# Twelve products instead of six to each addition in a squared-ReLU MLP

## The chip, the cores and the metric

The kernel runs on one core of a Trainium2 chip. Its time is the device time of one execution in microseconds (us); the figure of a kernel is the median of several executions. One execution is also taken by the hardware profiler, and its trace is what the views below are read from. The engines are PE (TensorE: matmuls; PEld is its loading of stationary operands), DVE (VectorE), ACT (ScalarE), POOL (GpSimd) and SP (SyncE, whose queue issues all DMAs here).

## The reference

One layer of a streaming encoder for 2048 prompt tokens and 32 sample tokens, model width 1024:

```python
def ffn_ple(h, p, g_mlp, w_up, w_down, w_ple_gate, w_ple_proj):
    c = rmsnorm(h, g_mlp)
    h = h + jnp.square(jax.nn.relu(c @ w_up)) @ w_down
    return h + jax.nn.sigmoid(h @ w_ple_gate) * (p @ w_ple_proj)
```

Ahead of it stand an RMSNorm, one input projection, two groups of attention heads (group A: differential attention over chunk-causal keys, group B: a band of nine chunks) and the output projection with its residual. After it comes a final RMSNorm. Everything is float32. `w_up` is 1024 x 4096 and `w_down` 4096 x 1024, so d_ff is 32 tiles of 128 and the width is 8 tiles of 128.

## The kernel before, in words

**Precision.** Each float32 operand is split into a high part (rounded to fp32r, by ACT: `wh`, `uh`, `cH`) and a low part (the difference, by POOL or DVE: `wl`, `ul`, `cL`). A product takes three matmuls: high by high, high by low, low by high (`mm3`, lines 256 to 262). These three lines, 260 to 262, stand for nearly all matmuls in the profile; the tiles tell them apart: `ups` for up products, `dps` for down products, `ops` for the output projection.

**Blocks.** The tokens are four blocks: 512, 544 (512 and the 32 sample tokens), 512 and 512. Block 1 is worked as two halves of 272 columns, the others as one of 512 (`SUBS`). Blocks 0 and 1 go through the MLP described here; blocks 2 and 3 go through another form of it later (`uphase`, `dphase`), which the change leaves alone.

**The MLP of a block** (`mlp`, `mlp_up`, `mlp_down`, lines 950 to 1015). d_ff is walked in 16 chunks of two tiles. A chunk's up part takes two weight units of 1024 rows by 128 columns: 24 matmuls for each token half into one PSUM bank, then ReLU and square on ACT (lines 972, 973) into a tile `tmp`, and the split into the two tiles `uh` and `ul`. Its down part takes two weight units of 256 rows by 512 columns. For each of the eight tiles of the width and each token half, six matmuls (two d_ff tiles, three each) go into one PSUM bank, and DVE adds the bank to the residual `h` (line 1001). The down part of a chunk follows the up part of the next one. Ups and downs of the output projection and the norm's sums share one ring of two PSUM banks, `mm`; from chunk 9 of block 1 on, the downs alternate between it and attention's banks.

**Order.** The program is written as generators that are woven together by hand; `mlp` yields after parts of a chunk, and other work (loading and normalizing the next block, the output projections of blocks 2 and 3, and so on) takes a step at each yield. When the kernel is built, a scheduler then lays down a fixed order for each engine from its own estimate of times; so the MLP of blocks 0 and 1, which stands behind attention in the program, fills PE beside the end of attention. On the chip each engine takes its instructions in that fixed order, SP its DMA issues too.

**Rings in SBUF that matter here.** `uq`, eight tiles for `uh` and `ul` (line 1597); `wh` and `wl`, three each, with three raw weight tiles; `tmp` in the pool `wk`, four tiles (`self.nt`, line 201), used for the residual's tiles in the output projection (`hd`, line 870), loads for the norms (`raw_o`, `cload`) and the ReLU's result; `r`, two tiles for the norms' factors (lines 851, 932); a separate `tmp` of seven tiles (`ox`, line 1601) for the work that is woven into block 1, `xnorm2` and `xnorm3` among it (their tiles are called `xe`). A tile of a ring can be taken again when all that read it are done.

Of the kernel before, what the change touches and what calls it, by code (L numbers as in the profile page):

```python
# [12 lines left out]
F32 = mybir.dt.float32  # L13
F32R = mybir.dt.float32r
AF = mybir.ActivationFunctionType
ALU = mybir.AluOpType
# [3 lines left out]
P = 128  # L20
# [69 lines left out]
def packed(w, rows, cols):  # L90
    k = rows // P
    n, m = w.shape[0] // rows, w.shape[1] // cols
    w = w.reshape(n, k, P, m, cols).transpose(0, 3, 2, 1, 4)
    return np.ascontiguousarray(w).reshape(n, m, P, k * cols)


def packed_weights(w):
    v = [w["w_in"][0, :, 1536 * g + 1024 : 1536 * g + 1536] for g in range(2)]
    qk = [w["w_in"][0, :, 1536 * g : 1536 * g + 1024] for g in range(2)]
    return {  # L100
        "w_v": np.stack([packed(x, 512, 256) for x in v]),
        "w_qk": np.stack([packed(x, 1024, P)[0] for x in qk]),
        "w_out": packed(w["w_out"][0], 1024, P)[0],
        "w_up": packed(w["w_up"][0], 1024, P)[0],
        "w_down": packed(w["w_down"][0], 256, 512),
        "w_ple_gate": packed(w["w_ple_gate"][0], 1024, P)[0],
        "w_ple_proj": packed(w["w_ple_proj"][0], 256, 512)[0],
    }
# [17 lines left out]
def drain(gen):  # L126
    for _ in gen:
        pass
# [67 lines left out]
class Kern:  # L196
    def __init__(self, tc, a):
        self.tc = tc
        self.nc = tc.nc
        self.a = a  # L200
        self.nt = 4
        self.nraw = 2
        self.pre = []

# [631 lines left out]
    def oload(self, b, wk, up, out):  # L836
        nc = self.nc
        n, t0 = BN[b], T0[b]
        if up.whole:
            oact = [up.tile([P, 8, up.aw], F32R, tag="act", name="oact") for _ in range(2)]  # L840
            oact = [[t[:, k, :n] for k in range(8)] for t in oact]
        else:
            oact = [[up.tile([P, up.aw], F32R, tag="u", name="ou")[:, :n] for k in range(8)] for _ in range(2)]
        out[b] = oact
        ahead = 1 if type(wk) is Mix else 0
        raws = []
        for k in range(8):
            while len(raws) <= min(k + ahead, 7):
                raws.append(self.raw_o(wk, len(raws), t0, n))
            if k == 4:  # L850
                r = wk.tile([P, BLK], F32, tag="r", bufs=2, name="rb")[:, :n]
                self.dma(r, self.rB[:, t0 : t0 + n])
            raw = raws[k]
            if k >= 4:
                nc.vector.scalar_tensor_tensor(
                    raw, raw, self.g_b[:, k - 4 : k - 3], r, op0=ALU.mult, op1=ALU.mult
                )
            self.split(oact[0][k], oact[1][k], raw, "act", "dve")
            yield
# [65 lines left out]
    def colnorm2(self, sq, b, scale, wk, tp, tag, dst, out):  # L925
        nc = self.nc
        n, t0, subs = BN[b], T0[b], SUBS[b]
        sh = wk.tile([P, BLK], F32R, tag="sh", bufs=1, name="sh")[:, :n]
        sl = wk.tile([P, BLK], F32R, tag="sl", bufs=1, name="sl")[:, :n]
        self.split(sh, sl, sq, "act", "dve")  # L930
        yield
        r = wk.tile([P, BLK], F32, tag="r", bufs=2, name="r")[:, :n]
        for s0, sn in subs:
            ss = tp.tile([P, 512], F32, tag=tag, name="css")[:, :sn]
            nc.tensor.matmul(ss, self.ones, sh[:, s0 : s0 + sn], start=True, stop=False)
            nc.tensor.matmul(ss, self.ones, sl[:, s0 : s0 + sn], start=False, stop=True)
            v = sq[:, s0 : s0 + sn]
            y = r[:, s0 : s0 + sn]
            nc.scalar.activation(v, ss, AF.Copy, scale=scale, bias=EPS)
            nc.scalar.activation(y, v, AF.Ln)  # L940
            nc.scalar.activation(y, y, AF.Exp, scale=-0.5)
            nc.vector.tensor_tensor(v, v, y, op=ALU.mult)
            nc.vector.tensor_tensor(v, v, y, op=ALU.mult)
            nc.vector.tensor_scalar(v, v, -0.5, 1.5, op0=ALU.mult, op1=ALU.add)
            nc.vector.tensor_tensor(y, y, v, op=ALU.mult)
        if dst is not None:
            self.dma(dst[:, t0 : t0 + n], r)
        out.append(r)

    def mlp_up(self, ch, nf, blocks, st, wk, up, mm, lo):  # L950
        nc = self.nc
        us, w = {}, {}
        order = [(f, b) for f in range(nf) for b in blocks]
        if ch == 0:
            order = [(f, b) for b in blocks for f in range(nf)]
        for f, b in order:
            ft = nf * ch + f
            if f not in w:
                w[f] = self.wunit(self.a["w_up"][ft], [8, P], "act", lo)
            wh, wl = w[f]  # L960
            h, cH, cL = st[b]
            uh = up.tile([P, up.aw], F32R, tag="u", name="uh")
            ul = up.tile([P, up.aw], F32R, tag="u", name="ul")
            us[f, b] = (uh, ul)
            for s0, sn in SUBS[b]:
                ps = mm.tile([P, 512], F32, tag="mm", name="ups")[:, :sn]
                self.mm3(
                    ps,
                    [(wh[:, k], wl[:, k], cH[:, k, s0 : s0 + sn], cL[:, k, s0 : s0 + sn]) for k in range(8)],
                )  # L970
                r = wk.tile([P, BLK], F32, tag="tmp", bufs=self.nt, name="relu")[:, :sn]
                nc.scalar.activation(r, ps, AF.Relu)
                nc.scalar.activation(r, r, AF.Square)
                self.split(uh[:, s0 : s0 + sn], ul[:, s0 : s0 + sn], r, "act", lo)
        return us

    def mlp_down(self, ch, nf, blocks, us, st, wk, mm, lo):
        nc = self.nc
        nd = 8 // nf
        for dh in range(nf):  # L980
            wh, wl = self.wunit(self.a["w_down"][ch, dh], [nf, P * nd], "act", lo)
            for d in range(nd):
                dd = nd * dh + d
                for b in blocks:
                    h = st[b][0]
                    for s0, sn in SUBS[b]:
                        ps = mm.tile([P, 512], F32, tag="mm", name="dps")[:, :sn]
                        self.mm3(
                            ps,
                            [  # L990
                                (
                                    wh[:, f, P * d : P * d + P],
                                    wl[:, f, P * d : P * d + P],
                                    us[f, b][0][:, s0 : s0 + sn],
                                    us[f, b][1][:, s0 : s0 + sn],
                                )
                                for f in range(nf)
                            ],
                        )
                        hv = h[dd][:, s0 : s0 + sn]  # L1000
                        nc.vector.tensor_tensor(hv, hv, ps, op=ALU.add)  # L1001
            yield

    def mlp(self, blocks, st, wk, up, mm, md, turn):
        nf = 2
        prev = None
        for ch in range(DFF // (P * nf)):
            lo = "pool" if ch < turn else "dve"
            us = self.mlp_up(ch, nf, blocks, st, wk, up, mm, lo)
            yield ch, 0  # L1010
            if prev is not None:
                for i, _ in enumerate(self.mlp_down(ch - 1, nf, blocks, prev, st, wk, md, lo)):
                    yield ch, 1 + i
            prev = us
        drain(self.mlp_down(ch, nf, blocks, prev, st, wk, md, lo))

    def tsplit(self, dst, src, lo_eng):
        self.split(dst[:, 0], dst[:, 1], src, "act", lo_eng)
# [458 lines left out]
    def run(self):  # L1477
        tc, nc, a = self.tc, self.nc, self.a
        with ExitStack() as top:
# [100 lines left out]
            with ExitStack() as x:  # L1580
                pool = opened(x, "a1", 1, side="right")
                for js in JA1:
                    self.attn_a(js, pool, ps_s, ps_t, ps_o)
            wk = opened(sq_, "wk", 1)
            acc, cn, st = {}, {}, {}
            def norms(b, act, ps):
# [7 lines left out]
                weave(self.outproj(0, wk, oa[0], mm, acc[0]), self.oload(1, wk, oq, oa), 1, 0, OW)  # L1594
                weave(self.outproj(1, wk, oa[1], mm, acc[1]), norms(0, actq, mm), 1, 1)
            hq = opened(sq_, "hq", 1)
            uq = Sized(opened(sq_, "uq", 8), BLK)
            rxs, oxs = ExitStack(), ExitStack()
            rx = Sized(opened(rxs, "rx", 5, side="right"), 512, True)
            ox = opened(oxs, "ox", 1, side="right")  # L1600
            wx = Mix(wk, tmp=(ox, 7))
            ps2 = Rings((ps_t, "tp"))
            X = {}

# [30 lines left out]
            for b in HALVES[0]:  # L1635
# [2 lines left out]
                h = [hq.tile([P, BLK], F32, tag="h", bufs=8, name="h") for _ in range(8)]  # L1638
                hmove(b, h, True)
                dn = Turn(mm)  # L1640
                m = self.mlp((b,), {b: (h,) + cn[b]}, wk, uq, mm, dn, (16, 11)[b])
                if b == 0:
                    next(m)
                    pre = self.cpre(1, wk, self.colnorm(acc[1][0], 1, 1.0 / D, wk, mm, "mm", None))
# [131 lines left out]
```

## Time and profile before

| | us |
|---|---|
| median of 3 runs | 2969.64 (2968.85 to 2970.52) |
| profiled execution | 2970.7 |
| its span, from first to last instruction | 2968.9 |

The granted TensorE clock was 0.994 of full speed over the span. A group's row in the profile reads: line, engine, operation, output <- inputs, shapes, count, then busy us and mean ns of one instruction, then the engine's idle time before the group's instructions and what ended it. A wait's row reads: who waited, for whom, us in total, times, longest. Ends of matmuls are modelled; their starts are measured.

### The profile page before, as it was taken

How to read it: one execution, taken by the hardware profiler on the slowest of the kernel's cores; microseconds unless marked ns; L12 is line 12 of the kernel's file. 1: busy time of each engine (PE TensorE's matmuls, PEld its weight loads, DVE VectorE, ACT ScalarE, POOL GpSimd, SP SyncE). 2: the span in 40 equal slices, each digit the busy share in tenths (PEclk: the TensorE clock that was granted, in tenths of full speed). 3: DMA queues.
4: the chain of work that ended last, by engine and by line, in shares of the span. 5: the costliest groups of instructions: out<-in, count | busy, mean ns of one | idle time of the engine just before them, and what ended most of it. 6: DMA issues, size and time to landing. Idle time of an engine off the chain costs nothing.

```text
span 2968.9 us, 49388 instructions
## 1 busy us (share of the span) xinstructions
PE 2902.3 (98%) x17027; PEld 2556.1 (86%) x17027; DVE 1847.5 (62%) x4120; ACT 1766.0 (59%) x3743; POOL 1386.8 (47%) x1903
## 2 busy tenths in 40 slices
PE   7899999999999999999999999999999999999998
PEld 6798998998889788888899999889888887888886
DVE  6565855444466554776767664376666666777955
ACT  5566757766567665776677764343444454455554
POOL 4677665533355445665564457620755533143000
PEclk9999999999999999999999999999999999999999
DMA  9877577876677644554654325563444486756711
GB/s 360 293 246 240 191 247 262 256 235 196 220 260 243 214 140 163 160 177 151 202 178 152 114 93 170 179 209 111 165 153 156 147 320 224 261 198 203 264 64 57
DMA packets 301370, 584.58 MB, mean 197 GB/s; under 512 B 34720, under 2 KB 132128, under 8 KB 301120
## 3 DMA queue, kind: packets, MB, share of 16 engines
q1 hardware_dynamic: 301120, 581.43, 58.5%
q8 instruction: 135, 2.21, 0.3%
q14 instruction: 115, 0.94, 0.1%
HBM read 450.10 MB, written 131.22 MB: 196 GB/s over the span
## 4 chain that ended last, share of the span: by engine, by line
PE 89%; DVE 5%; DMA 2%; ACT 2%; issue 1%; POOL 1%; SPq 0%; ACTq 0%; DVEq 0%; POOLq 0%
PE ups L260 4%; PE ups L261 4%; PE ups L262 4%; PE qps L261 4%; PE qps L260 4%; PE s L590 4%; PE qps L262 4%; PE dp L260 4%; PE dp L261 4%; PE dp L262 4%; PE dps L260 4%; PE xps L262 3%; PE xps L261 3%; PE xps L260 3%; PE dps L262 3%; PE dps L261 3%
## 5 line engine op out<-in xcount | busy, mean ns | idle before, releaser
L229 POOL TENSOR_TENSOR wl<-wr,wh 128x256 fp32r<-128x256 f32 x736 | 552.1, 781 | 527.2 <-ACT wh L234 458.9
L234 ACT ACTIVATE wh<-wr 128x1024 fp32r<-128x1024 f32 x270 | 284.9, 1056 | 229.6 <-PE dps L261 52.6
L260 PE MATMUL dps<-uh,wh 128*128 128x272 f32 (+1 forms) x768 | 255.6, 333 | 11.2 <-DVE h L1001 10.2
L260 PE MATMUL ups<-cH,wh 128*128 128x272 f32 (+1 forms) x768 | 249.7, 325 | 0.6 <-DVE h L1001 0.5
L261 PE MATMUL ups<-cL,wh 128*128 128x272 f32 (+1 forms) x768 | 249.1, 324 | 0.0
L262 PE MATMUL ups<-cH,wl 128*128 128x272 f32 (+1 forms) x768 | 249.1, 324 | 0.0
L262 PE MATMUL dps<-uh,wl 128*128 128x272 f32 (+1 forms) x768 | 247.9, 323 | 0.0
L261 PE MATMUL dps<-ul,wh 128*128 128x272 f32 (+1 forms) x768 | 247.5, 322 | 0.0
L1001 DVE TENSOR_TENSOR h<-h,dps 128x272 f32<-128x272 f32 (+1 forms) x384 | 194.9, 516 | 73.8 <-PE dps L262 72.0
L260 PE MATMUL qps<-aH,wh 128*128 128x512 f32 (+3 forms) x640 | 228.8, 358 | 0.0
L261 PE MATMUL qps<-aL,wh 128*128 128x512 f32 (+3 forms) x640 | 227.9, 356 | 0.0
L262 PE MATMUL qps<-aH,wl 128*128 128x512 f32 (+3 forms) x640 | 227.6, 356 | 0.0
L219 POOL TENSOR_TENSOR wl<-wr,wh 128x256 fp32r<-128x256 f32 x208 | 154.2, 773 | 118.5 <-ACT wh L234 115.4
L261 PE MATMUL dp<-dx,dw 128*128 128x512 f32 x448 | 178.1, 397 | 0.0
L590 PE MATMUL s<-ka,q 128*128 128x512 f32 (+3 forms) x640 | 174.5, 367 | 2.1 <-DVE nm L599 0.8
L262 PE MATMUL dp<-dx,dw 128*128 128x512 f32 x448 | 175.2, 397 | 0.0
L260 PE MATMUL dp<-dx,dw 128*128 128x512 f32 x448 | 167.7, 398 | 4.6 <-ACT dx L234 4.6
L260 PEld LDWEIGHTS dps<-uh,wh 128*128 128x128 f32 x768 | 144.3, 188 | 30.2 <-DVE h L1001 19.1
L771 DVE CUSTOM_DVE_ANT_0 eb<-sb,bb 128x320 f32<-128x320 f32 (+2 forms) x232 | 104.3, 479 | 99.0 <-PE tpb L783 97.0
L1114 POOL TENSOR_TENSOR wc<-wq,wc 128x256 fp32r<-128x256 f32 x96 | 91.8, 977 | 157.2 <-ACT wc L1111 157.1
L260 PE MATMUL vps<-wh,aH 128*128 128x256 f32 (+1 forms) x544 | 156.6, 290 | 6.5 <-ACT aH L234 5.1
L673 DVE TENSOR_TENSOR pL<-tpp,pH 128x512 fp32r<-128x512 f32 (+5 forms) x168 | 95.9, 584 | 100.4 <-ACT pH L672 99.4
(269 smaller groups left out, 9222.6 us busy)
## 6 DMA issues: line engine op xcount, KB each, us to landing
wd<-w_down SPq DMA_DIRECT2D x96, 512.0 KB, 5.3
q<-qS SPq DMA_DIRECT2D x128, 256.0 KB, 4.0
v<-vSa SPq DMA_DIRECT2D x64, 512.0 KB, 4.0
wr<-w_up SPq DMA_DIRECT2D x64, 512.0 KB, 3.7
wr<-w_down SPq DMA_DIRECT2D x64, 512.0 KB, 3.7
wr<-w_qk SPq DMA_DIRECT2D x58, 512.0 KB, 4.7
ut<-uS SPq DMA_DIRECT2D x56, 512.0 KB, 4.3
qS<-qk SPq DMA_DIRECT2D x32, 512.0 KB, 3.7
```

Of the source, the lines that this page charges most:

```text
L219: nc.gpsimd.tensor_tensor(out[:, sl], a[:, sl], b[:, sl], op=op)
L229: nc.gpsimd.tensor_tensor(out[:, sl], a[:, sl], b[:, sl], op=op)
L234: nc.scalar.activation(hi, raw, AF.Copy)
L260: nc.tensor.matmul(ps, lh, rh, start=start and i == 0, stop=False)
L261: nc.tensor.matmul(ps, lh, rl, start=False, stop=False)
L262: nc.tensor.matmul(ps, ll, rh, start=False, stop=stop and i == n - 1)
L590: nc.tensor.matmul(s, q[:, m, hl, P * qi : P * qi + nr], kt[:, m, k0 - kb : k0 - kb + n], start=hl == 0, stop=hl == 1)
L673: nc.vector.tensor_tensor(l_, s_, h_.bitcast(F32), op=ALU.subtract)
L771: nc.vector.tensor_tensor_reduce(e[:, w * i : w * i + w], s, bb[:nr, b0 + w * i : b0 + w * i + w], 1.0, -3e38, ALU.add, ALU.max, st[:, 3 + ...
L1001: nc.vector.tensor_tensor(hv, hv, ps, op=ALU.add)
L1114: nc.gpsimd.tensor_tensor(w[:, 1, sl], src[:, sl], w[:, 0, sl].bitcast(F32), op=ALU.subtract)
```

## The change

The MLP of a block is worked by four d_ff tiles at a time. A down group has 12 matmuls (four d_ff tiles, three each) before DVE adds its bank to `h`. The down weights are packed a second time, as units of 512 rows by 256 columns (`w_down4`; `w_down` stays for the later blocks); a unit has 512 KB as before, and a block still takes 32 up and 32 down units. The order is five ups, four downs, then four ups and four downs in turn; at the end three ups and four downs. The yields fall after the same numbers of units as before. The ring of `uh` and `ul` grows from 8 to 10 tiles; in exchange `tmp` shrinks from 4 to 3, `r` from 2 to 1 (both from the output projection of block 0 on) and the separate `tmp` from 7 to 6.

```diff
@@ packed_weights
+        "w_down4": packed(w["w_down"][0], 512, 256),
@@ Kern.__init__
-        self.nt = 4
+        self.nt, self.nr = 4, 2
@@ oload, colnorm2
-                r = wk.tile([P, BLK], F32, tag="r", bufs=2, name="rb")[:, :n]
+                r = wk.tile([P, BLK], F32, tag="r", bufs=self.nr, name="rb")[:, :n]
...
+    def mlp_up(self, f, b, st, wk, up, mm, lo):
+        nc = self.nc
+        wh, wl = self.wunit(self.a["w_up"][f], [8, P], "act", lo)
...
+    def mlp_down(self, c, q, b, us, st, mm, lo):
+        nc = self.nc
+        wh, wl = self.wunit(self.a["w_down4"][c, q], [4, 2 * P], "act", lo)
+        for d in range(2):
+            h = st[0][2 * q + d]
+            sl = slice(P * d, P * d + P)
             for s0, sn in SUBS[b]:
-                ps = mm.tile([P, 512], F32, tag="mm", name="ups")[:, :sn]
+                ps = mm.tile([P, 512], F32, tag="mm", name="dps")[:, :sn]
                 self.mm3(
                     ps,
-                    [(wh[:, k], wl[:, k], cH[:, k, s0 : s0 + sn], cL[:, k, s0 : s0 + sn]) for k in range(8)],
+                    [
+                        (wh[:, f, sl], wl[:, f, sl], us[4 * c + f][0][:, s0 : s0 + sn], us[4 * c + f][1][:, s0 : s0 + sn])
+                        for f in range(4)
+                    ],
                 )
...
+                hv = h[:, s0 : s0 + sn]
+                nc.vector.tensor_tensor(hv, hv, ps, op=ALU.add)
+
+    def mlp(self, b, st, wk, up, mm, md, turn):
+        nf = DFF // P
+        units = [(f, None) for f in range(5)]
+        for c in range(nf // 4):
+            units += [(c, q) for q in range(4)]
+            units += [(f, None) for f in range(4 * c + 5, min(4 * c + 9, nf))]
+        us = {}
+        for i, (x, q) in enumerate(units):
+            ch, part = divmod(i + 2, 4)
             lo = "pool" if ch < turn else "dve"
-            us = self.mlp_up(ch, nf, blocks, st, wk, up, mm, lo)
...
+            if q is None:
+                us[x] = self.mlp_up(x, b, st, wk, up, mm, lo)
+            else:
+                self.mlp_down(x, q, b, us, st, md, lo)
+            if ch < 16 and part and (ch, part) != (0, 2):
+                yield ch, (part - 1) * (ch > 0)
@@ run
+            self.nt, self.nr = 3, 1
             wk = opened(sq_, "wk", 1)
...
-            uq = Sized(opened(sq_, "uq", 8), BLK)
+            uq = Sized(opened(sq_, "uq", 10), BLK)
...
-            wx = Mix(wk, tmp=(ox, 7))
+            wx = Mix(wk, tmp=(ox, 6))
...
-                m = self.mlp((b,), {b: (h,) + cn[b]}, wk, uq, mm, dn, (16, 11)[b])
+                m = self.mlp(b, (h,) + cn[b], wk, uq, mm, dn, (16, 11)[b])
```

More of the change, by code (lines that the diff above doesn't have):

```diff
@@ L931, in colnorm2 @@
         yield
-        r = wk.tile([P, BLK], F32, tag="r", bufs=2, name="r")[:, :n]
+        r = wk.tile([P, BLK], F32, tag="r", bufs=self.nr, name="r")[:, :n]
         for s0, sn in subs:
@@ L948, in colnorm2 @@
         out.append(r)
-    def mlp_up(self, ch, nf, blocks, st, wk, up, mm, lo):
+    def mlp_up(self, f, b, st, wk, up, mm, lo):
         nc = self.nc
[L952 to L964, printed above, removed]
+        wh, wl = self.wunit(self.a["w_up"][f], [8, P], "act", lo)
+        h, cH, cL = st
+        uh = up.tile([P, up.aw], F32R, tag="u", name="uh")
+        ul = up.tile([P, up.aw], F32R, tag="u", name="ul")
+        for s0, sn in SUBS[b]:
+            ps = mm.tile([P, 512], F32, tag="mm", name="ups")[:, :sn]
+            self.mm3(
+                ps,
+                [(wh[:, k], wl[:, k], cH[:, k, s0 : s0 + sn], cL[:, k, s0 : s0 + sn]) for k in range(8)],
+            )
+            r = wk.tile([P, BLK], F32, tag="tmp", bufs=self.nt, name="relu")[:, :sn]
+            nc.scalar.activation(r, ps, AF.Relu)
+            nc.scalar.activation(r, r, AF.Square)
+            self.split(uh[:, s0 : s0 + sn], ul[:, s0 : s0 + sn], r, "act", lo)
+        return uh, ul
@@ L971, in mlp_up @@
[L971 to L1007, printed above, removed]
-            lo = "pool" if ch < turn else "dve"
-            us = self.mlp_up(ch, nf, blocks, st, wk, up, mm, lo)
[L1010 to L1015, printed above, removed]
+                    [
+                        (wh[:, f, sl], wl[:, f, sl], us[4 * c + f][0][:, s0 : s0 + sn], us[4 * c + f][1][:, s0 : s0 + sn])
+                        for f in range(4)
+                    ],
+                )
```

## The prediction

> **What bounds the kernel now.** I read the engine totals first, then the busy time by stretch, then TensorE's waits, then its matmuls by shape.
>
> ```profile
> span 2968.9 us, 49388 instructions
> PE 2902.3 (98%) x17027; PEld 2556.1 (86%) x17027; DVE 1847.5 (62%) x4120; ACT 1766.0 (59%) x3743; POOL 1386.8 (47%) x1903
> ```
>
> PE (TensorE) is busy for 98% of the span, no other engine for more than 62%. An edit that takes work off DVE, ACT or POOL is therefore worth only the PE idle time that this work caused. Columns of the next view: stretch, its length, busy time of PE, PEld, DVE, ACT, POOL, granted clock, DMA share, GB/s.
>
> ```profile
> 815.00:960.00 145.00, 143.02 (x950) 131.76 (x949) 91.38 (x266) 101.84 (x189) 75.76 (x105) 0.99 0.75 249
> 960.00:2090.00 1130.00, 1113.81 (x6945) 1002.57 (x6944) 705.40 (x1530) 695.21 (x1478) 557.88 (x785) 1.00 0.50 162
> 1980.00:2010.00 30.00, 26.46 (x201) 25.15 (x200) 30.00 (x56) 14.65 (x27) 0.00 (x0) 1.00 0.60 195
> ```
>
> The MLP of blocks 0 and 1 runs from 960 to 2090 us, woven with the last of the attention: the program order is one thing, the order laid down at build time fills attention's gaps on PE with MLP matmuls. PE idles 1130 - 1113.8 = 16.2 us there, at a full clock. 3.5 us of it lie in 1980 to 2010, where DVE is busy for 30.00 of 30.00 us. Now PE's own waits there, then its weight loads':
>
> ```profile
> PE dps L260 <- DVE h L1001: 10.2, 18, 1.5
> ```
> ```profile
> PEld dps L260 <- DVE h L1001: 19.1, 29, 1.7
> ```
>
> Two thirds of the idle time is one wait: the first matmul of a down group (tile dps) waits until DVE has added an older group to h (L1001) and so freed its PSUM bank. This is the wait that the change touches. A break costs more than its gap:
>
> ```profile
> 1457.89 0.50 PE L260 MATMUL dps<-uh,wh 128*128 128x512 f32 x1 [0.21 <-DVE h L1001]
> 1458.23 0.39 PE L261 MATMUL dps<-ul,wh 128*128 128x512 f32 x1
> 1458.45 0.40 PE L262 MATMUL dps<-uh,wl 128*128 128x512 f32 x1
> ```
>
> In a stream, starts of 512-column matmuls lie 0.22 to 0.23 us apart (last two rows); the one after the break lasts 0.50 instead of 0.39, and the next starts 0.34 later. So part of the loss is booked as busy, and the groups by shape show it (count, busy us, mean ns, idle before):
>
> ```profile
> L260 PE MATMUL dps<-uh,wh 128*128 128x272 f32 x512 | 151.6, 297 | 8.3 <-DVE h L1001 8.0
> L260 PE MATMUL ups<-cH,wh 128*128 128x272 f32 x512 | 148.0, 289 | 0.5 <-DVE h L1001 0.5
> L260 PE MATMUL dps<-uh,wh 128*128 128x512 f32 x256 | 104.0, 406 | 2.8 <-DVE h L1001 2.3 <-ACT relu L972 0.4
> L260 PE MATMUL ups<-cH,wh 128*128 128x512 f32 x256 | 101.7, 397 | 0.0
> ```
>
> The up matmuls (24 to a group) are the same work without the wait. Against them the down matmuls lose 8.3 + 2.8 = 11.1 us idle and (151.6 - 148.0) + (104.0 - 101.7) = 5.9 us of slow firsts: 17.0 us is what adding after six products costs PE now.
>
> **The change part by part.** *Products.* Down groups go from 6 to 12 matmuls and from 384 to 192; 384 x 6 = 192 x 12 = 2304 matmuls of the same shapes, so PE's work is equal.
>
> ```profile
> L1001 DVE TENSOR_TENSOR h<-h,dps 128x272 f32<-128x272 f32 x256 | 107.8, 433 | 43.5 <-PE dps L262 42.9
> L1001 DVE TENSOR_TENSOR h<-h,dps 128x512 f32<-128x512 f32 x128 | 87.1, 681 | 30.3 <-PE dps L262 29.2
> ```
>
> DVE loses half of 194.9 us of adds, 97 us, none of it on the path except through those waits. First, half of the group starts are gone, and with them half of the 17.0 us: -8.5. Second, the remaining groups cover more. While an add waits for its turn on DVE, PE works on the other bank: 6 x 0.23 = 1.4 us of 512-column matmuls, or 6 x 0.125 = 0.75 us of 272-column ones, whose starts lie 0.125 us apart (eight steps in 1.00 us from the first of these rows to the last):
>
> ```profile
> 1499.83 0.29 PE L260 MATMUL ups<-cH,wh 128*128 128x272 f32 x1
> ...
> 1500.83 0.29 PE L262 MATMUL ups<-cH,wl 128*128 128x272 f32 x1
> ```
>
> This cover doubles. The 29 waits above last 19.1 / 29 = 0.66 us on average and 1.7 at most, the added cover is 0.75 to 1.4 us, so most of the rest falls too; bounds 0 and -8.5, I take -5.5. Both together: -14.0. What is late next at these places is attention's own waits, which PE already pays. One place I hold back: in 1980 to 2010 DVE has no free time, so half of those 3.5 us should stay, where the two steps above took 14/17 of them: +1.1.
>
> *Order.* Four ups, then four downs, one up ahead, instead of two and two. Weight units keep their number and size.
>
> ```profile
> L234 ACT ACTIVATE wh<-wr 128x1024 fp32r<-128x1024 f32 x142 | 150.1, 1057 | 149.3 <-PE dps L261 52.6 <-PE ups L261 37.1 <-PE ops L261 29.6
> ...
> L234 ACT ACTIVATE uh<-relu 128x512 fp32r<-128x512 f32 x32 | 20.3, 634 | 0.5
> L973 ACT ACTIVATE relu<-relu 128x512 f32<-128x512 f32 x32 | 20.1, 628 | 0.3
> L972 ACT ACTIVATE relu<-ups 128x512 f32<-128x512 f32 x32 | 18.6, 581 | 0.0
> ```
> ```profile
> L219 POOL TENSOR_TENSOR wl<-wr,wh 128x256 fp32r<-128x256 f32 x208 | 154.2, 773 | 118.5 <-ACT wh L234 115.4 <-DMA tmp<-cB 2.0 <-PE s L590 1.1
> L219 POOL TENSOR_TENSOR ul<-relu,uh 128x256 fp32r<-128x256 f32 x64 | 49.1, 788 | 5.8 <-ACT uh L234 5.7
> ```
>
> The low half of a down unit stays four pieces of 256 columns on POOL, at 773 ns: nothing. In a run of ups of block 0, POOL needs 4 x 0.77 + 2 x 0.79 = 4.7 us and ACT 1.06 + 0.58 + 0.63 + 0.63 = 2.9 us a unit, against 24 x 0.23 = 5.5 us of PE without attention and more with it; so a longer run does not overtake them: 0, and if attention's share of ACT comes in bursts, up to about 1 us in each of 8 runs. The lead of one up holds except for the last four tiles of a block, where the downs follow up 31 at once. PE reaches the fourth term after 9 x 0.23 = 2.1 us; the tile takes 0.58 + 0.63 + 0.63 + 1.58 = 3.4 us: +1.3 in block 0. In block 1 the two halves of 272 leave the first one ready in time: 0. With ten tiles of u the fifth pair is written while the four older ones are read, and up 4c+5 writes after down c has left PE: 0.
>
> *Smaller rings.* tmp goes from 4 to 3, r from 2 to 1, the side ring from 7 to 6. All of it sits on SP's queue, which issues in order: a load that waits for its slot holds weights and attention's q behind it. The uses of r follow one another in the program: 0. Of tmp, three places matter. KB and median us from issue to landing:
>
> ```profile
> hd<-xT SPq DMA_DIRECT2D x24, 256.0 KB, 3.8
> hS<-hd SPq DMA_DIRECT2D x24, 256.0 KB, 2.8
> ...
> hd<-xT SPq DMA_DIRECT2D x8, 272.0 KB, 3.3
> hS<-hd SPq DMA_DIRECT2D x8, 272.0 KB, 2.6
> ...
> tmp<-cB SPq DMA_DIRECT2D x8, 272.0 KB, 4.2
> ```
> ```profile
> 857.00 0.69 DVE L884 TENSOR_TENSOR hd<-hd,ops 128x512 f32<-128x512 f32 x1
> ...
> 887.67 0.68 DVE L884 TENSOR_TENSOR hd<-hd,ops 128x512 f32<-128x512 f32 x1
> ...
> 905.78 0.43 DVE L884 TENSOR_TENSOR hd<-hd,ops 128x272 f32<-128x272 f32 x1
> ...
> 959.48 0.42 DVE L884 TENSOR_TENSOR hd<-hd,ops 128x272 f32<-128x272 f32 x1
> ```
>
> In outproj of blocks 0 and 1 a step takes hd, tmp and oraw (or a norm's tile) in turn, so with three slots the load of hd d+1 waits for the store of hd d: 0.7 + 2.8 + 3.8 = 7.3 us in block 0 and 0.4 + 2.6 + 3.3 = 6.3 in block 1, against steps of (887.67 - 857.00)/4 = 7.7 and (959.48 - 905.78)/6 = 8.95 us now. It fits, barely in block 0, where a free PSUM bank covers one late load: I take 0, bounds 0 and, without attention beside it, the second rival's price. Between blocks, the eight loads of block 1's norm come three at a time instead of four: each holds its slot for 4.2 us of landing and a split on ACT and DVE of 0.6 to 0.7 us each (as uh and the add of 512 columns), 5.5 us, so 8 x 5.5/3 = 15 us instead of 11, inside four down units of 22 us; DVE's queue can be held by one of them: +1, bounds 0 and +4. The side ring's six tiles are as many as xnorm3 has in use at once, so a load may have to wait for a store, at about hd's 2.8 + 3.8 = 6.6 us, in each of its four steps, with the adds queued behind it on DVE; the program leaves 24 us of PE to a step, so I take 0 beyond the 1.1 held back above, bounds 0 and, less 3 us of cover from two banks of 12 matmuls, 4 x 3.6 = +14.
>
> Sum: -14.0 + 1.1 + 1.3 + 1.0 = -10.6 us. The profiled execution took 2970.7 us (span 2968.9 and 1.8 around it), 1.06 above the median of 2969.64. So 2960.1 profiled, **2959.0 us** as a median.
>
> **The rivals.** *The waits are DVE's queue, not the group's length.* Where an add stands behind one or two 0.7 us instructions of attention, a longer group may only move the wait. Then the starts saved count in part and the cover nothing, and the ring's costs eat the rest: a gain of 0 to 5.9 us, about 2967. For it: waits of up to 1.7 us, longer than the cover. Against: the mean of 0.66 is under it. The Trainium skill, Perfetto Trace Analysis, in Optimizing Tensor Performance, says that groups which rotate through PSUM banks have their evacuation overlapped by the next group's matmuls; by that rule nothing would be saved and the time stays at 2969.6. The trace disagrees in part: the groups rotate, and 10.2 us of waits remain. Chance 0.22.
>
> *The store-to-load chain in outproj becomes the pace (slower).* Only attention beside it makes the steps of outproj longer than the chain. If the new order moves attention away, PE needs 24 x 0.23 = 5.5 us (block 0) or 48 x 0.125 = 6.0 us a step: 8 x (7.3 - 5.5) + 8 x (6.3 - 6.0) = 17 us lost at median landings, 2976. It outweighs the gain by over 0.2% once steps average under 5.8 us (8 x 1.5 + 8 x 0.5 = 16). Against it: 7.7 and 8.95 us now, and no edit before outproj but the rings. The same page, in Optimization Strategy, says that a gap repeating on the engine that should be full can mean too little SBUF for the next tile; such a gap is what this would show. Chance 0.08, with 0.04 more for a worse order elsewhere.
>
> That the change doesn't do what it says is hardly possible: halving the adds is in its text.
>
> **How the numbers follow.** 0.2% is 5.9 us, about what a measurement of this kernel can tell from no change. The forecast case, a gain of 6 us to everything PE loses there (16.2 + 5.9 = 22 us, 2947.5), has 0.66; no change 0.22; slower 0.12. The range goes from 2948 to 2976, from all that PE loses there to the outproj rival. The forecast's own is 2948 to 2963.7, where the gain is 5.9 us.
>
> **What would show it.** Right: 192 instructions on the add's line, DVE 97 us less busy, PE's wait of dps for h under 3 us and dps firsts as short as ups'; PE's busy time 4 to 6 us lower. Wrong: the same waits in sum with fewer and longer pieces (first rival); in 815 to 960 more than 2.0 us idle with SP waiting on stores of hd (second); a matmul wait for relu or u at a block's end over 2 us; DVE waiting on loads of xe near 1980.

## The result and the profile after

The changed kernel takes 2983.28 us, the median of 5 runs (2982.68 to 2988.17). The kernel before took 2969.85 on the same chip (2968.85 to 2971.33). The ratio is 1.0047, its 95% interval 1.0033 to 1.0061: slower by 13.4 us where 10.6 us less had been forecast. The profiled execution has a span of 2981.1 us, 12.2 more than before.

First the page of the kernel after: the engine totals, and TensorE (PE) with its granted clock in 40 slices of 74.5 us.

```profile
span 2981.1 us, 49216 instructions
PE 2903.8 (97%) x17027; PEld 2561.3 (86%) x17027; DVE 1766.3 (59%) x3930; ACT 1762.1 (59%) x3743; POOL 1368.8 (46%) x1895
...
PE   7899999999999999999999997999999999999998
...
PEclk9999999999999999999999997999999999999999
```

The matmuls are as many as before. The 25th slice (1789 to 1863 us) shows 7 in both rows: there PE has gaps and runs at a lower clock. The page of before has a 9 in every slice of the clock. The stretches, with the columns of the prediction's view (stretch, length, PE, PEld, DVE, ACT, POOL, clock, DMA share, GB/s); 1780 to 1860 first from before, then from after:

```profile
1780.00:1860.00 80.00, 78.80 (x501) 71.75 (x500) 32.12 (x54) 32.76 (x55) 57.50 (x81) 1.00 0.52 173
```
```profile
815.00:960.00 145.00, 142.08 (x946) 129.81 (x945) 89.35 (x259) 100.58 (x188) 75.16 (x106) 1.00 0.75 245
960.00:2090.00 1130.00, 1103.70 (x6861) 998.07 (x6859) 614.91 (x1330) 691.02 (x1476) 541.18 (x776) 0.98 0.49 161
1780.00:1860.00 80.00, 59.05 (x299) 48.75 (x298) 34.42 (x68) 40.60 (x90) 28.30 (x44) 0.81 0.40 127
1980.00:2010.00 30.00, 30.00 (x229) 29.32 (x228) 22.88 (x39) 10.76 (x14) 2.77 (x4) 1.00 0.54 172
```

In 960 to 2090 PE now idles 1130 - 1103.7 = 26.3 us instead of 16.2. In 1780 to 1860 alone it idles 80 - 59.05 = 20.95 instead of 1.2, so in all the rest only 5.3 instead of 15.0. Outside this stretch the change did what was forecast, and PE's waits say so (who waited, for whom, us, times, longest; the first two lie inside it):

```profile
PE ops L261 <- ACT oact L235: 8.9, 1, 8.9
PE tpp L666 <- DVE e L630: 4.6, 1, 4.6
PE dps L261 <- DVE h L985: 3.5, 3, 2.1
```
The wait of the down groups for the adds has gone from 10.2 us in 18 pieces to 3.5 in 3. The groups by shape (count, busy, mean ns, idle before; the lines of the file have moved):

```profile
L261 PE MATMUL ups<-cH,wh 128*128 128x272 f32 x512 | 147.7, 289 | 0.0
L261 PE MATMUL dps<-uh,wh 128*128 128x272 f32 x512 | 147.4, 289 | 1.4 <-DVE h L985 1.4
L261 PE MATMUL dps<-uh,wh 128*128 128x512 f32 x256 | 102.0, 399 | 2.2 <-DVE h L985 2.1
L261 PE MATMUL ups<-cH,wh 128*128 128x512 f32 x256 | 101.0, 395 | 0.0
...
L985 DVE TENSOR_TENSOR h<-h,dps 128x272 f32<-128x272 f32 x128 | 54.8, 433 | 48.6 <-PE dps L263 47.9
L985 DVE TENSOR_TENSOR h<-h,dps 128x512 f32<-128x512 f32 x64 | 43.5, 681 | 48.4 <-PE dps L263 48.3
```

The down matmuls lose (147.4 - 147.7) + (102.0 - 101.0) + 1.4 + 2.2 = 4.3 us where they lost 17.0. The adds are halved, 98.3 us instead of 194.9.

What is new is at 1795. PE's timeline there:

```profile
1795.02 0.29 PE L263 MATMUL ups<-cH,wl 128*128 128x272 f32 x1
...
1798.84 3.18 PE L591 MATMUL s<-ka,q 128*128 128x512 f32 x6 [2.40 <-ACT e L604]
...
1806.65 1.97 PE L666 MATMUL tpp<-ident,e 128*128 128x128 f32 x8 [4.63 <-DVE e L630]
...
1824.94 0.58 PE L692 MATMUL ss<-sl,ones_r 128*128 128x256 f32 x1 [0.16 <-POOL sl L220]
...
1834.45 1.22 PE L261 MATMUL ops<-oact,wh 128*128 128x512 f32 x2 [8.93 <-ACT oact L235]
1835.46 0.63 PE L262 MATMUL ops<-oact,wh 128*128 128x512 f32 x1
1835.89 0.63 PE L263 MATMUL ops<-oact,wl 128*128 128x512 f32 x1
...
1840.51 0.39 PE L262 MATMUL ops<-oact,wh 128*128 128x512 f32 x1
1840.74 0.40 PE L263 MATMUL ops<-oact,wl 128*128 128x512 f32 x1
```

After 1795.02 no matmul of the MLP stands between those of attention (tiles `s`, `tpp`, `o`, `ss`); PE waits for each softmax step in the open until attention ends at 1825.5. Then the next matmuls are `ops`: the output projection of block 2, the first side work of block 1 that needs attention's result. The chain of waits across that gap:

```profile
1829.83 0.50 DVE os L694
1830.34 0.33 SPq L211
1830.72 2.96 DMA oraw<-oT
1833.76 0.64 ACT oact L235
1834.45 1.22 PE ops L261 x2
```

Attention's last output is scaled, stored, loaded, rounded, and only then multiplied: 8.9 us in which PE has nothing else in its order. In the kernel before the same chain ran too, but MLP matmuls covered it: attention ended at 1778.3, `ops` began at 1791.85, and the row of 1780 to 1860 above shows 1.2 us idle.

For a balance I took the distance between the starts of each two successive matmuls and subtracted the usual distance (the median in the kernel before) for that shape. What is left is PE's loss: gaps, slow firsts and slow clock together. It sums to 84.8 us before and 97.2 after, a difference of 12.4 for 12.2 us of span. That the sums agree follows from how they are made, since all kernels have the same 17027 matmuls; what the table tells is where the time went. "Later side" and the others are experiments told below.

| us lost in | before | after | later side | six products | short rings |
|---|---|---|---|---|---|
| 0 to 815 | 39.4 | 37.4 | 39.2 | 38.9 | 41.8 |
| 815 to 960 | 4.7 | 5.7 | 5.8 | 5.2 | 5.2 |
| 960 to 1480 | 8.8 | 4.5 | 2.6 | 16.1 | 13.1 |
| 1480 to 1780 | 10.4 | 3.7 | 2.6 | 16.1 | 10.1 |
| 1780 to 1860 | 2.2 | 31.9 | 4.1 | 8.5 | 1.7 |
| 1860 to 2100 | 6.7 | 0.8 | 1.5 | 10.7 | 9.5 |
| after 2100 | 12.5 | 13.1 | 13.1 | 12.7 | 12.5 |
| all | 84.8 | 97.2 | 69.1 | 108.2 | 93.9 |
| at down matmuls | 19.3 | 4.0 | 4.0 | 32.7 | 19.2 |

### The profile page after: what moved, and what is told of

The parts are those of the page before. It is cut to its first block, busy times and chain, and to the rows that moved or that the text cites. A ratio compares the mean times of both kernels' runs of the same rounds, so it can differ in the third digit from the quotient of the medians.

```text
span 2981.1 us, 49216 instructions
## 1 busy us (share of the span) xinstructions
PE 2903.8 (97%) x17027; PEld 2561.3 (86%) x17027; DVE 1766.3 (59%) x3930; ACT 1762.1 (59%) x3743; POOL 1368.8 (46%) x1895
## 5 line engine op out<-in xcount | busy, mean ns | idle before, releaser
L230 POOL TENSOR_TENSOR wl<-wr,wh 128x256 fp32r<-128x256 f32 x936 | 694.4, 773 | 676.8 <-ACT wh L235 607.4
L261 PE MATMUL dps<-uh,wh 128*128 128x272 f32 (+1 forms) x768 | 249.5, 326 | 3.5 <-DVE h L985 3.5
L597 DVE TENSOR_REDUCE nm<-s 128x1 f32<-128x512 f32 (+1 forms) x192 | 121.5, 640 | 59.6 <-PE s L591 58.5
L263 PE MATMUL vps<-wh,aL 128*128 128x256 f32 (+1 forms) x544 | 155.5, 288 | 1.1 <-DVE aL L241 1.1
L262 PE MATMUL vps<-wl,aH 128*128 128x256 f32 (+1 forms) x544 | 155.1, 288 | 1.2 <-DVE wl L241 1.2
```

Of the source, the lines that this page charges most:

```text
L230: nc.gpsimd.tensor_tensor(out[:, sl], a[:, sl], b[:, sl], op=op)
L261: nc.tensor.matmul(ps, lh, rh, start=start and i == 0, stop=False)
L262: nc.tensor.matmul(ps, lh, rl, start=False, stop=False)
L263: nc.tensor.matmul(ps, ll, rh, start=False, stop=stop and i == n - 1)
L597: nc.vector.tensor_reduce(nmx, s, axis=AX.X, op=ALU.max, negate=True)
```

## The theories

**The order.** With 12-product groups the order laid down at build gives the MLP more of PE early, and the MLP gets ahead of attention. How far it may go is set by the side work: block 1's MLP cannot go far past the point in the program at which the side work needs attention's output. It reaches its stop while attention still has 91 matmuls to do, and attention's tail then has no filler. The lead is in the trace. Busy PE, PEld and DVE from 955 to 1780 of the up tiles, then the down tiles, of before:

```profile
955.00:1780.00 825.00, 298.02 (x1536) 243.01 (x1536) 31.01 (x64) 1.00 0.49 160
955.00:1780.00 825.00, 297.50 (x1419) 229.75 (x1420) 132.93 (x236) 1.00 0.49 160
```

and of after:

```profile
955.00:1780.00 825.00, 318.21 (x1662) 262.03 (x1662) 32.77 (x68) 1.00 0.49 160
955.00:1780.00 825.00, 299.59 (x1536) 243.91 (x1536) 71.09 (x128) 1.00 0.49 160
```

By 1780 the MLP has done 126 up and 117 down matmuls more than before, and attention has its last ones still to do. The ups then stop at 1728, the downs stand at 1536: of block 0 all 32 + 32 units and of block 1 36 of 64, at 24 matmuls to a unit of block 0 and 48 of block 1. The lead is one of order, not of speed: counted by attention's own 3912 matmuls (tiles `s`, `tpp`, `o`, `ss`, `sb`, `tpb`, `ob`) instead of by time, 2376 MLP matmuls stand ahead of its 300th from the last in the kernel before and 2873 in the one after.

What stops the MLP can be read from the weight loads. SP's loads into the ring of raw tiles and ACT's roundings out of it follow each other one for one (208 loads and 205 roundings up to the stop, three raw tiles), so a rounding can be told by its load. For three of the last six roundings ahead of the stop that is a load of `w_out`, the output projection's weights: the loads of 1720.09, 1735.77 and 1767.59, rounded at 1743.52, 1763.62 and 1795.38. The third load, its rounding and the next one:

```profile
1767.59 0.34 SPq L211 DMA_DIRECT2D wr<-w_out  x1
```
```profile
1795.38 1.06 ACT L235 ACTIVATE wh<-wr 128x1024 fp32r<-128x1024 f32 x1
...
1847.96 2.01 ACT L235 ACTIVATE wh<-wr 128x1024 fp32r<-128x1024 f32 x2
```

No `ops` runs before 1834.45. So from 1795.4 on all three tiles of `wh` hold weights that wait for attention's output, and the MLP's next ones, loaded at 1788.56, have no tile until `ops` has given one back.

**Rivals.** The smaller rings make the time, and the gap at 1800 is only where it shows. Or the switch of the down groups to attention's PSUM banks in chunk 9 of block 1, not the side work, stops the MLP. Or side work that comes later is a gain in any kernel, whatever the groups.

## The experiments

Ratios are to the kernel before on the same chip, with 95% intervals; its median there was 2971.86 us for the runs with six products, the short rings and the side work one and two chunks later in the kernel after, 2970.74 for the last two runs, and 2971.80 for the other four.

**Side work two chunks later.** The side work keeps its steps; they start in chunk 9 instead of 7.

```diff
-SIDE = {**{i: (2, 2, 1) for i in range(7, 12)}, **{i: (1, 1, 0) for i in range(12, 16)}}
+SIDE = {**{i: (2, 2, 1) for i in range(9, 14)}, **{i: (2, 1, 1) for i in range(14, 16)}}
```

> The changed kernel, with the woven-in side work (loading, projecting and normalizing blocks 2 and 3) starting two chunks later in block 1's MLP. Theory A (order): the MLP, laid down by longer groups, ran ahead of attention, reached the side work, which needs attention's output, and left attention's last 30 us without filler; with eight units more ahead of that point PE's 21 us of idle time in 1780 to 1980 fall to under 3 and the half clock there goes too: 2957 to 2963 us. Theory B (rings): the loads of the side work come late because tmp and r are short; then moving their place in the program does not help: 2980 us or more. Theory C (long groups hold up attention's own matmuls on PE): 2980 us or more as well, with attention ending near 1825.

Measured: 2954.37 us, ratio 0.9935 [0.9921, 0.9948], faster than both kernels and 2.6 us below the range expected. Its page, and its row for 1780 to 1860:

```profile
PE 2892.1 (98%) x17027; PEld 2553.6 (86%) x17027; DVE 1758.4 (60%) x3930; ACT 1761.2 (60%) x3743; POOL 1371.8 (46%) x1895
```
```profile
1780.00:1860.00 80.00, 77.23 (x585) 74.79 (x585) 39.50 (x81) 46.31 (x105) 35.28 (x55) 1.00 0.40 131
```

The clock is at 1.00 again and 585 matmuls stand where 299 stood. Attention ends later still, at 1841.8, and that costs nothing, since the MLP now fills it: the third rounding of `w_out` comes at 1866.56, after the first `ops` at 1855.20, so the ring of `wh` is never full of them. So attention's late end isn't the price; the missing filler is.

**Side work one chunk later.** The same by one chunk.

```diff
-SIDE = {**{i: (2, 2, 1) for i in range(7, 12)}, **{i: (1, 1, 0) for i in range(12, 16)}}
+SIDE = {**{i: (2, 2, 1) for i in range(8, 13)}, **{i: (1, 1, 1) for i in range(13, 16)}}
```

> The changed kernel, with the side work one chunk later, so four units (24 us of PE) more ahead of it. Theory A: the stretch without filler was some 30 us of attention's tail, 21 us of it idle; four units nearly fill it: 2958 to 2966 us, PE idle in 1780 to 1980 under 6 us. Theories B and C: 2980 us or more.

Measured: 2972.56 us, 0.9999 [0.9991, 1.0008]: part of the gain only. The row and the wait:

```profile
1780.00:1860.00 80.00, 67.30 (x461) 62.48 (x460) 39.73 (x80) 43.17 (x96) 32.59 (x50) 0.91 0.41 132
```
```profile
PE ops L261 <- ACT oact L235: 8.8, 1, 8.8
```

The MLP now comes to 1776 ups and 1680 downs before the stop, exactly four units of 48 further than after (1728 and 1536: 48 + 144 = 192). The tail of the softmax is filled, the store and load before `ops` is not: attention ends at 1838.5 and the 8.8 us are whole. Three roundings of `w_out` (1788.22, 1804.50, 1830.93) fill the ring of `wh` again, and the next rounding is at 1859.36. The stop follows `SIDE` by its chunk, and one chunk is not enough; I had taken it to be nearly so.

**Side work three chunks later.** Also in the kernel after.

```diff
-SIDE = {**{i: (2, 2, 1) for i in range(7, 12)}, **{i: (1, 1, 0) for i in range(12, 16)}}
+SIDE = {i: (2, 2, 2) for i in range(10, 16)}
```

> The changed kernel with the side work three chunks later and two steps at each of the last 18 yields. Theory A: e1 lost 4 us in 1780 to 1860, so at most some 3 more are to be had there; the side work's 33 steps are crowded into six chunks, DVE is full longer before 2100 and gives part back: 2951 to 2960 us.

Measured: 2954.08 us, 0.9936 [0.9922, 0.9950]. PE is full in the stretch, and the time is that of two chunks:

```profile
1780.00:1860.00 80.00, 80.00 (x630) 79.12 (x629) 38.93 (x78) 48.71 (x110) 36.15 (x58) 1.00 0.38 127
```

Two chunks are enough; getting back the 4.1 us lost there with two made no measurable difference.

**The later side work in the kernel before.** Only this line is changed, all else is as before.

```diff
-SIDE = {**{i: (2, 2, 1) for i in range(7, 12)}, **{i: (1, 1, 0) for i in range(12, 16)}}
+SIDE = {**{i: (2, 2, 1) for i in range(9, 14)}, **{i: (2, 1, 1) for i in range(14, 16)}}
```

> The kernel before the change with the side work two chunks later, as in e1. Theory A (the MLP's filler runs out at the side work in the changed kernel alone): before the change filler was left when attention ended, so the place gains nothing there: within 4 us of the kernel before, unless the later start crowds the end of the MLP. Theory E (a late start of the side work is better by itself, and e1's gain has nothing to do with the change): 10 to 20 us faster than the kernel before, as e1 was.

Measured: 2976.43 us, 1.0015 [1.0006, 1.0023]. It gains nothing, it costs 4.6 us. So the later side is no improvement by itself: it only takes away what the change brought about at 1800. With the side work late in both, the change is worth 2976.43 - 2954.37 = 22.1 us.

**The bank switch two chunks later.** In the kernel after, the down groups get attention's banks later.

```diff
-                        if ch == 9 and part == 0:
+                        if ch == 11 and part == 0:
```

> The changed kernel with only the down groups' use of attention's PSUM banks starting at chunk 11 instead of 9. Theory A1 (the MLP stops at the side work's weights, which take the ring of three weight tiles): no change, 2980 to 2986 us, PE's wait of ops for oact of some 9 us still there. Theory A2 (it stops at the first down group that takes a bank attention still holds): the tail is filled, 2960 us.

Measured: 2984.24 us, 1.0040 [1.0025, 1.0054], the same as after, and the gap is there:

```profile
1780.00:1860.00 80.00, 58.76 (x314) 48.86 (x313) 34.96 (x69) 40.59 (x90) 28.86 (x44) 0.85 0.41 134
```

The MLP stops at the same unit. The switch isn't the stop.

**Six products again, in the new order.** The kernel after, with its order, weights and rings, but two groups of six and two adds instead of one of twelve.

```diff
-                ps = mm.tile([P, 512], F32, tag="mm", name="dps")[:, :sn]
...
-                        for f in range(4)
...
+                for f0 in (0, 2):
+                    ps = mm.tile([P, 512], F32, tag="mm", name="dps")[:, :sn]
...
+                            for f in range(f0, f0 + 2)
...
+                    hv = h[:, s0 : s0 + sn]
+                    nc.vector.tensor_tensor(hv, hv, ps, op=ALU.add)
```

> The changed kernel with its order of units, its weight units and its rings, but each down group broken in two of six products, with an addition each as before the change. Theory A: the length of the groups is what gave the MLP its lead; attention ends near 1780 to 1800 again with MLP work left ahead of the side work, the adds' waits of some 17 us are back: 2966 to 2976 us. Theory B (rings) and a theory D (the order of four ups and four downs is the cause): the loss stays and the waits come on top, 2990 us or more.

Measured: 2992.41 us, 1.0062 [1.0049, 1.0076]. Its up and down tiles to 1780, and its wait for the adds:

```profile
955.00:1780.00 825.00, 294.95 (x1508) 240.39 (x1509) 30.14 (x62) 1.00 0.48 158
955.00:1780.00 825.00, 288.41 (x1344) 218.15 (x1344) 127.65 (x224) 1.00 0.48 158
```
```profile
PE dps L261 <- DVE h L986: 14.0, 21, 2.2
```

The lead is gone (1508 and 1344 against 1662 and 1536), attention ends at 1774.3, and PE has no gap like that at 1800. By attention's count 2262 MLP matmuls stand ahead of its 300th from the last, fewer than before. So it is the length of the groups that gives the MLP its lead, not the order of units, nor the rings. The time missed the expectation by 16 us all the same, and lies where it was expected if the rings or the order of units were the cause; but the loss at 1800 that was to stay with them is not there (8.5 us in the table against 31.9). The waits on the adds are larger than in the kernel before (at down matmuls 32.7 us lost in the table, against 19.3). The new units and rings are no neutral ground: without the longer groups they cost. Some 7 of the 20.5 us are the rings' by the next run; what makes the rest wasn't separated.

**The smaller rings alone.** The kernel before, with `tmp` 3, `r` 1 and the side's `tmp` 6.

```diff
+            self.nt, self.nr = 3, 1
             wk = opened(sq_, "wk", 1)
...
-            wx = Mix(wk, tmp=(ox, 7))
+            wx = Mix(wk, tmp=(ox, 6))
```

> The kernel before the change with only the three rings shortened (tmp 4 to 3, r 2 to 1, the side work's tmp 7 to 6). Theory A: within 3 us of the kernel before, 2967 to 2973 us, PE idle in 815 to 960 about 2 us. Theory B: 2980 us or more, with PE waiting for oact or hd after attention's end as in the changed kernel.

Measured: 2978.60 us, 1.0021 [1.0012, 1.0030]: the rings cost the kernel before some 7 us, more than the 3 that I had allowed. They leave the order alone (2376 MLP matmuls ahead of attention's 300th from the last, as before). In 960 to 1130 and in 1980 to 2100, before and then with the short rings:

```profile
960.00:1130.00 170.00, 165.98 (x915) 141.64 (x914) 92.18 (x277) 113.72 (x217) 81.69 (x112) 1.00 0.52 170
1980.00:2100.00 120.00, 116.26 (x860) 111.75 (x859) 83.19 (x154) 48.91 (x89) 12.20 (x15) 1.00 0.46 151
```
```profile
960.00:1130.00 170.00, 164.65 (x898) 140.43 (x897) 92.49 (x284) 111.95 (x213) 76.66 (x106) 0.99 0.51 169
1980.00:2100.00 120.00, 114.68 (x872) 112.24 (x871) 82.75 (x155) 44.33 (x81) 3.10 (x5) 0.99 0.42 141
```

PE idles 1.3 and 1.6 us more there. In the table the loss is 4.3 us larger in 960 to 1480 and 2.8 in 1860 to 2100, where the rings are in use. (The 2.4 more ahead of 815 lie ahead of them: the columns differ there by up to 4.4 whatever was changed.) It is a cost of its own, and no part of the 30 us at 1800.

**Four tiles for `tmp`, with the later side.** The two-chunk version with one tile more.

```diff
-            self.nt, self.nr = 3, 1
+            self.nt, self.nr = 4, 1
```

> The kernel of e1 (side work two chunks later) with the ring tmp back at four tiles, r at one and the side work's tmp at six. e4 showed that the three short rings cost the kernel before some 7 us; if tmp is the one that costs, this is 2 to 5 us faster than e1, 2949 to 2953 us; if the side work's ring or the order they lead to is, it is within 2 us of e1.

Measured: 3259.93 us, 1.0969 [1.0953, 1.0986], some 300 us more than either outcome expected. The up and down tiles from 955 to 1300:

```profile
955.00:1300.00 345.00, 29.76 (x120) 22.01 (x120) 2.32 (x4) 0.83 0.43 140
955.00:1300.00 345.00, 0.00 (x0) 0.00 (x0) 0.00 (x0) 0.83 0.43 140
```

Here stand the five ups of block 0 (5 x 24 = 120) and no down at all, where the kernel after has 600 and 483. Attention runs with almost no filler, at a clock of 0.83.

**Two tiles for `r`, with the later side.** Was it `tmp`, or any tile more? Here `tmp` stays at 3.

```diff
-            self.nt, self.nr = 3, 1
+            self.nt, self.nr = 3, 2
```

> Side work later, with the second tile of r back and one tile taken from the side's weight ring, so that the left side of SBUF holds one tile more than in the run with the later side alone (2954.4) and one less than in the run with four addition tiles (3259.9, which took its tiles for the adds). If the footprint is what undoes the weave of MLP and attention: about 3150 to 3270, with hardly any down matmul before 1300. If it was the tile of the adds itself: 2950 to 2960. By what r is worth alone (under 2 us in the run with the short rings): no less than 2950.

The expectation counts the tiles wrongly: by its edit this run has as many in that pool as the one with four for `tmp`, one more than the two-chunk version, and the side's `tmp` stays at six.

Measured: 3272.21 us in the one run; 955 to 1300 again, the ups:

```profile
955.00:1300.00 345.00, 29.75 (x120) 22.05 (x120) 1.73 (x3) 0.82 0.43 141
```

The same collapse from another ring of that pool, so it is one tile more in it, whichever ring takes it. The two tiles taken from `tmp` and `r` pay for the two that the ring of u got, and there is none to spare. That with one more the MLP's pools come to lie where attention's buffers still stand is argued from where the pools are opened; no view shows addresses.

**Seven tiles for the side's `tmp`, with the later side.** This pool is opened on the other side of SBUF.

```diff
-            wx = Mix(wk, tmp=(ox, 6))
+            wx = Mix(wk, tmp=(ox, 7))
```

> Side work later, with the seventh tile of the side's weight ring back and nothing else. If the side ring costs what was left over in the run with the short rings (up to 3 us in the stretch after 1980 and ahead of 815): 2950 to 2953. If it cost nothing there and the adds' three tiles did: 2953 to 2956, no difference that can be measured. If this tile too makes the footprint too large: above 3100.

Measured: 2956.76 us, 0.9946 [0.9930, 0.9963], no different from the two-chunk version: its executions lie from 2953.32 to 2958.21, those of that version from 2951.45 to 2954.82. (The two were measured on different chips, each beside the kernel before, and the intervals of the ratios overlap.) There is room on that side, and nothing to be had for it.

## Why the prediction was wrong, point by point

- **Half the group starts gone and double the cover, -14.0: right.** At down matmuls PE lost 19.3 us before and 4.0 after and with the later side: -15.3. What each of the two halves gave wasn't measured apart. The first rival, that the waits were DVE's queue, is out. The Trainium skill, Perfetto Trace Analysis, in Optimizing Tensor Performance, has groups that rotate through PSUM banks overlap their evacuation with the next group. Groups of six fell short of that here (10.2 us of waits), groups of twelve come close (3.5 us).
- **Adds, -97 us of DVE: right**, 96.6 by the groups. The page's DVE total fell by only 81.2, since it counts what overlaps once.
- **Half of the wait in 1980 to 2010 held back, +1.1: too careful.** PE is busy for 30.00 of 30.00 us there, and DVE for 22.88 where it had been 30.00.
- **Order, "so a longer run does not overtake them: 0": this step failed.** I weighed the new order only by POOL and ACT within a run of units, and took the order between MLP and attention as it was. The build lays that down anew, and the longer groups moved it: 243 MLP matmuls more by 1780, then no filler for attention's tail, and a loss of 31.9 us instead of 2.2 in 1780 to 1860, of which 20.95 are idle and the rest slow clock and slow firsts. This one term is larger than all the gain. The 0.04 that I gave to "a worse order elsewhere", without place or price, is where the result fell.
- **The end of block 0, +1.3: did not show.** No wait of a down group for the ReLU or u is among PE's waits of after; its weight loads waited 0.2 us for them.
- **`tmp`, `r` and the side ring, +1 between blocks and 0 elsewhere: too small for the old groups; for the new, their cost wasn't measured apart.** Alone they cost some 7 us. With twelve products the losses of 960 to 1480 and 1860 to 2100 are under those of before, so their cost doesn't show there. That the room which the adds leave on DVE takes it up isn't shown: with twelve products only the side ring was tried at its old length without the collapse.
- **The second rival, outproj's chain as the pace: not so.** In 815 to 960 PE idles 2.9 us instead of 2.0, and loses 5.7 instead of 4.7, where that rival needed 17. Its sign did come up, more than 2.0 us idle with SP waiting on stores of hd: SP waited 17.3 us for them in 12 pieces there instead of 1.7 in 2. The queue waited on the chain, then, and PE lost 1.0 us more.
- **What would show it.** Short firsts of dps came out as asked, and the wait for h was 3.5 us, where under 3 was said. PE's busy time was to fall by 4 to 6 us; it rose by 1.5, since matmuls at the low clock are booked as busy (the 512-column ones after 1835 for 0.63 us each instead of 0.40). With the later side it is 10.2 us lower.

With the stop moved out of the way the change gives 17.5 us (2954.37 against 2971.86, ratio 0.9921 to 0.9948). Of this the table has 15.3 at the down matmuls. Why the scheduler gives longer groups the lead wasn't tried: the runs show that it does, not by what reckoning.

## What to carry to other kernels

Where an order is laid down at build from estimates, a change in the length of one instruction group is a change to the whole order: ask how far each stream may run ahead of the others and what stops it, and who fills the gaps of the stream that is left alone. A stretch that was covered before the change is worth a term of the sum for its loss of cover, even if no edit touches it. And if a change makes the profile better everywhere but at one place, look for the fixed point in the program (here a list of chunks) that was set for the old pace.

## What the runs showed of the hardware

PE's granted clock fell at gaps of 2.40 and 1.65 us, and came back late. Four stretches of the kernel after (the columns as above, the clock third from the right):

```profile
1796.00:1799.00 3.00, 0.60 (x6) 0.37 (x4) 2.32 (x4) 3.00 (x9) 2.49 (x4) 1.00 0.00 0
1800.00:1806.00 6.00, 1.95 (x4) 0.51 (x3) 3.34 (x13) 4.83 (x15) 4.21 (x8) 0.50 0.28 87
1814.00:1823.00 9.00, 6.62 (x46) 5.61 (x46) 2.66 (x5) 2.05 (x5) 0.00 (x0) 1.00 0.27 93
1824.00:1834.00 10.00, 1.13 (x2) 0.57 (x2) 0.56 (x2) 1.45 (x4) 3.30 (x5) 0.50 0.25 75
```

The clock is at 1.00 up to 1799, where a gap of 2.40 us has just ended (1798.84), and at 0.50 in 1800 to 1806. It is back at 1.00 in 1814 to 1823 and down again by 1824, inside a gap of 1.65 us (ended at 1824.22) and ahead of the one of 8.9. After that gap the matmuls of 512 columns started 0.43 us apart (1835.46 to 1835.89) instead of 0.23 (1840.51 to 1840.74), and the change came at 1840.2 to 1840.5, 5.7 to 6 us after the first of them. The Trainium skill, TensorE: Matmul & The Clock Gate, section "What's actually happening", gives two rates, half and full: half after an idle window of about 3.4 us, full after at least one busy window of that length. The distances of 0.43 and 0.23 agree with the two rates, and the 5.7 to 6 us of the way back with "at least one". The way down differs: the gaps here were 2.40 and 1.65 us, with matmuls on both sides, and neither fall came at an idle stretch of 3.4 us.
